# Hybrid trunk on one core: hi and lo of a moving operand side by side, and low parts of weights made by adding transfers

## The chip, the cores and the metric

The kernel runs on one core of a Trainium2 chip. Its engines have queues of their own: TensorE (PE; its weight loads are shown apart as PEld), VectorE (DVE), ScalarE (ACT), GpSimd (POOL) and SyncE (SP), which here only issues transfers (DMA). The metric is device time in microseconds (us), the median of several executions. The profile is of one execution, and counts times from the start of its span.

## The reference

Two layers of an encoder trunk over 256 frames of width 1024. In each layer a normed input is projected once, and the columns are shared out among three mixers and their gates:

```python
h = _rms(x, norm_g[l])
proj = h @ w_in[l]
y_a = _gla(gq, gk, gv, ga, ...) * silu(gz)
y_b = _dsa(bq, bk, bv, iq, ik, iw, ...) * silu(bz)
y_c = _diff(cq, ck, cv, ...) * silu(cz)
g = sigmoid(gate)
merged = g0 * (y_a @ w_br0) + g1 * (y_b @ w_br1) + g2 * (y_c @ w_br2)
x = x + merged @ w_out[l]
```

`_gla` is gated linear attention in chunks of 64 frames: a state per head is updated from keys and values (`state` in the kernel) and read by the queries (`go`). `_dsa` scores keys with a small indexer, keeps the top 64 for each query and attends over them. `_diff` takes the difference of two softmaxes and applies it to values (`av`). All is float32.

## The kernel before

**Two numbers for one.** A float32 product is made of three products in a reduced format: each operand is split into hi (rounded) and lo (what is left), and hi·hi, hi·lo and lo·hi are summed in PSUM. `mm3` issues the three matmuls. A split is one ACT copy that rounds and one DVE subtraction: `split` for activations, `Stream.split` (lines 165 to 170) for weights.

**Weights.** All weights are cut into units of 128 partitions x 1024 numbers (512 KB), 92 per layer, in the order `ORDER` names them: four units for a block of 512 projected columns, six for `br0` and `br1` (the three branches' output projections, one half of the width each), two for each `out` block. `Stream.load` issues a unit's transfer on SP's queue into one of 5 raw buffers; `Stream.split` makes its hi (`whi`) on ACT and its lo (`wlo`) on DVE, each in one of 6 buffers, so that a unit can be split only when PE has finished the unit six back.

**The main line and the tasks.** `project` walks a block's units: for each, two slices of 128 rows, and for each slice three matmuls of 512 columns for each half of the 256 frames (`t` = 0, 1), six in all, and then one `flow.pump()`. `project_T` (for `iq` and `bz`) makes the transposed product with 256 moving columns: for each of four blocks of output columns it walks all four units, so that these four are free late. The rest of a layer (norms, logits, softmax, top-k, the state, the gated read) is written as tasks, Python generators that `flow.pump()` lets go one step at a time; the table `Y` says after how many pumps a step follows. `flow.until` pumps until a result needed by the main line (`y0`, `y1`, `y2` of the branches) is there. A planner orders each engine's instructions from modelled durations and hands out buffers; a task's matmuls may come later than the main line's matmul at which they were issued, not earlier.

**Buffers.** SBUF tiles of one tag share a number of slots: `kp` (27 slots of 128x512) holds gates, value tiles, split queries, the y tiles and the merged output; `w2` (6) is for short-lived work. PSUM has two tags of four banks each: `pj` for projections, `at` for the tasks.

**What the change touches.** `av` (line 608) multiplies the transposed probabilities with cv for each head and block of keys. `gla_task` (line 803) makes the state for each half, splits it into S, then makes `go`, whose squares and scaling give `ya`. `dsa_out` (line 663) is the other use of values; it has its own matmuls and isn't changed. `val[c]` (line 935) splits bv, cv and gv after their projection. `branches` (line 873) takes br0 or br1, branch by branch in the order 0, 2, 1, and frees three gates.

Of the kernel before, what the change touches and what calls it, by code (L numbers as in the profile page):

```python
# [8 lines left out]
F32 = mybir.dt.float32  # L9
F32R = mybir.dt.float32r  # L10
BF16 = mybir.dt.bfloat16
AF = mybir.ActivationFunctionType
OP = mybir.AluOpType
# [5 lines left out]
P = 128  # L19
NOSYNC = mybir.DependencyInfo(mybir.DependencyClass.NoSync, mybir.DependencyReason.DATA)  # L20
CH = 512
# [9 lines left out]
COL = dict(gq=0, gk=256, gv=512, ga=1024, gz=1040, bq=1552, bk=2064, bv=2576, iq=3088, ik=3600,  # L31
           iw=3664, bz=3672, cq=4184, ck=4696, cv=5208, cz=5720, gate=6232)
ORDER = ["bq", "cq", "ck", "gate2", "cz", "bk", "cv", "gq", "iq", "bv", "gv", "gz", "bz", "gate0", "gate3",
         "gate4", "gate5", "br0", "gate1", "br1", "out00", "out10", "out01", "out11"]
BRANCHES = (0, 2, 1)
UNIT, NUNIT = {}, 0
for _c in ORDER:
    UNIT[_c] = NUNIT
    NUNIT += 2 * NB if _c.startswith("br") else 2 if _c.startswith("out") else 4

def columns(*widths):
    at, res = 0, {}
    for name, w in widths:
# [10 lines left out]
MERGE_WAIT = 4  # L56
WARM = 14
AHEAD1 = (0, 2)
Y = dict(sm0=0, qk0=1, qk=3, dsa0=6, dec0=8, diff0=1, gla0=0, att0=3, top=1, blog=6, bpT=11, by=3, clog=4,
         cpT=2, cy=2, za=17, q2=5, st=27, go=9)  # L60
BUFS = dict(w2=6, kp=27, w4=6, ev=2, raw=5, wt=6, ahead=21)


@with_exitstack
def trunk(ctx: ExitStack, tc: tile.TileContext, x0, x1, units, wsmall, pack, ptmp, wa2b, out):
    nc = tc.nc
    V, A, G = nc.vector, nc.scalar, nc.gpsimd

    class Tensor:


        chained, last = False, None
# [14 lines left out]
    TE = Tensor()  # L87
# [3 lines left out]
    sp = ctx.enter_context(tc.tile_pool(name="sp", bufs=1))  # L91
# [4 lines left out]
    def nm(s):  # L96
        cnt[0] += 1
        return f"{s}_{cnt[0]}"

    def w2(shape, dt=F32, n="w2"):  # L100
        return sp.tile(shape, dt, tag="w2", bufs=BUFS["w2"], name=nm(n))

# [15 lines left out]
    def at(shape, n="at"):  # L118
        return pp.tile(shape, F32, tag="at", bufs=4, name=nm(n))
# [22 lines left out]
    class Stream:  # L142
# [22 lines left out]
        def split(self):  # L165
            j = len(self.made)
            raw, (hi, lo) = self.raws[j], self.tiles()
            self.splits[j] = (A.activation(hi, raw, AF.Copy), V.tensor_sub(lo, raw, hi.bitcast(F32)))  # L168
            if j in self.after:
                self.hold(j, self.after[j])  # L170

# [41 lines left out]
    def mm3(ps, lh, ll, rh, rl, first, last):  # L213
        TE.matmul(ps, lh, rh, start=first, stop=False)
        TE.matmul(ps, lh, rl, start=False, stop=False)
        TE.matmul(ps, ll, rh, start=False, stop=last)

    def rstd(ss, n, dim):
        v, r = tiny(n, "v"), tiny(n, "r")
# [163 lines left out]
    ps = pj([P, CH], "idle")  # L383
# [11 lines left out]
    last = {}  # L395
# [7 lines left out]
    wt = [ws.tiles() for _ in range(4)]  # L403
# [53 lines left out]
    r = scale(1)  # L457
# [6 lines left out]
    for l in range(L):  # L464
# [13 lines left out]
        def cq_task(mark, ps, dst):  # L478
            n = headnorm(ps, 8, 64)
            yield Y["qk"]  # L480
            ps, gain = transposed(n), gains[:, L + l:L + l + 1]
# [7 lines left out]
        def ck_task(mark, ps, tt):  # L489
            n = headnorm(ps, 8, 64)  # L490
            yield Y["qk"]
            ps, gain = transposed(n), pkc("dkg", l, l + 1)
# [7 lines left out]
        def qk_task(mark, ps, nh, dh, gain, hi, lo):  # L500
            n = headnorm(ps, nh, dh)
            yield Y["qk"]
            qkT(n, gain, hi, lo)
# [103 lines left out]

        def av(pT, vs, t):

            o = at([P, 4, P], "av")  # L610
            for h in range(4):
                hs = slice(h * P, h * P + P)
                for s in range(t + 1):
                    mm3(o[:, h], *pT[h][s], vs[s][0][:, hs], vs[s][1][:, hs], s == 0, s == t)
            return o

        def transposed_probs(pt, h0, per, t, pT):

# [127 lines left out]
        Es, kd, q2T = [], [], []  # L746
# [56 lines left out]
        def gla_task():  # L803
            carry = None
            S, o = [], []
            for t in range(2):
                sps = at([P, 4, P], "state")
                for h in range(4):
                    lh = kd[t][0][:, h].rearrange("p c d -> p (c d)")
                    ll = kd[t][1][:, h].rearrange("p c d -> p (c d)")  # L810
                    hs = slice(h * P, h * P + P)
                    mm3(sps[:, h], lh, ll, val["gv"][t][0][:, hs], val["gv"][t][1][:, hs], True, True)
                if t == 0:
                    carry = w2([P, 4, P], F32, "carry")
                    A.activation(carry[0:64], sps[64:P], AF.Copy)
                    A.activation(carry[64:P], sps[64:P], AF.Copy)
                    S.append(split(sps, [P, 4, P], "S"))
                else:
                    sd = w2([P, 4, P], F32, "sd")
                    V.tensor_tensor(sd, carry, decay.unsqueeze(2).to_broadcast([P, 4, P]), op=OP.mult)  # L820
                    V.tensor_tensor(sd, sps, sd, op=OP.add)
                    S.append(split(sd, [P, 4, P], "S"))
                yield 1
            ys = []
            for t in range(2):
                yield 1
                o = at([P, 4, P], "go")
                for h in range(4):
                    mm3(o[:, h], q2T[t][0][:, h], q2T[t][1][:, h], S[t][0][:, h], S[t][1][:, h], True, True)
                ss = tiny(4, "ss")  # L830
                junk = w2([P, CH], F32, "junk")
                for h in range(4):
                    A.activation(junk[:, h * P:(h + 1) * P], o[:, h], AF.Square, scale=0.125, accum_out=ss[:, h:h + 1])
                r = rstd(ss, 4, 128)
                f = tiny(4, "f")
                V.tensor_scalar_mul(f, r, 0.125 * 0.5)
                y = w2([P, CH], F32, "ya")
                for h in range(4):
                    hs = slice(h * P, h * P + P)
                    V.scalar_tensor_tensor(y[:, hs], o[:, h], f[:, h:h + 1], val["gz"][t][:, hs], op0=OP.mult, op1=OP.mult)  # L840
                ys.append(y)
            for t in range(2):
                yield Y["go"]
                yTs[0, t] = yT(ys[t])
                flow.done.add(f"y0{t}")


        notsel, val, th, mT = {}, {}, {}, {}
        bpT = [[w4([P, 4, T], F32R, "bpT") for _ in range(2)], [w2([P, 4, P], F32R, "bpT") for _ in range(2)]]
# [44 lines left out]
        for c in ORDER:  # L894
            if c.startswith("out"):
                break
            if c.startswith("br"):
                branches(int(c[2]))
                continue
            if c == "bz":  # L900
                val[c] = [silu2(ps.rearrange("p j t -> p (j t)"), c) for ps in project_T(c)]
                flow.done.add(c)
                continue
            if c == "iq":
                iqT = [split_iq(ps) for ps in project_T(c)]
                flow.done.add(c)
                continue
            ps_ = next(firsts) if c in ORDER[:2] else proj(c, base)
            if c == "bq":
                with ExitStack() as behind:  # L910
                    if l == 0:
                        for e in "AV":
                            behind.enter_context(tc.issue_after(last[e].ins))
                    load_small()
                    if l == 0:
                        constants()
                flow.start(small_task(), Y["sm0"])
            if c in heads:
                nh, dh, gain, dst = heads[c]
                for t in range(2):  # L920
                    flow.start(qk_task(f"{c}{t}", ps_[t], nh, dh, gain, *dst[t]), Y["qk0"])
            elif c == "cq":
                for t in range(2):
                    flow.start(cq_task(f"{c}{t}", ps_[t], cqT[t]), Y["qk0"])
            elif c == "ck":
                for t in range(2):
                    flow.start(ck_task(f"{c}{t}", ps_[t], tts[t]), Y["qk0"])
            elif c == "gq":
                flow.start(gqk_task(ps_), 0, {"dec"})
            elif c.startswith("gate"):  # L930
                for t in range(2):
                    th[int(c[4]), t] = kp([P, CH], F32, "gate")
                    A.activation(th[int(c[4]), t], ps_[t], AF.Tanh, scale=0.5)
            elif c[1] == "v":
                val[c] = [split(ps, [P, CH], c, kp) for ps in ps_]
                flow.done.add(c)
            else:
                val[c] = [silu2(ps, c) for ps in ps_]
                if c == "gz":
                    for g in val[c]:  # L940
                        g3 = g.rearrange("p (h d) -> p h d", h=4)
                        G.tensor_tensor(g3, g3, pkc("glag", l * P, l * P + P).unsqueeze(1).to_broadcast([P, 4, P]),
                                        op=OP.mult)
                flow.done.add(c)
# [3 lines left out]
        for h, n, t in ((0, 0, 0), (0, 0, 1), (0, 1, 0), (0, 1, 1), (1, 0, 0), (1, 1, 0), (1, 0, 1), (1, 1, 1)):  # L948
# [3 lines left out]
            for ps, c in cols:  # L952
                for k in range(4):
                    wh, wl = ws.need(base + UNIT[f"out{n}{h}"] + k // 2)
                    hi, lo = mT[h, t]
# [90 lines left out]
```

## Time and profile before

| | |
|---|---|
| median of 3 runs | 601.77 us (601.76 to 601.82) |
| profiled execution, its own time | 601.7 us |
| its span | 599.8 us |
| busy: PE, weight loads, DVE, ACT, POOL | 593.6, 504.4, 438.6, 348.8, 66.5 us |
| HBM read, written | 99.23, 1.05 MB |

The span is what the rows of the profile cover; the execution's own time is some 2 us longer. A row names line, engine, operation, and what is written from what (out<-in, without buffer numbers; for a matmul the moving operand and then the stationary one). "xN" counts instructions, "busy" sums their durations, "mean" is one instruction's, and what follows the bar's second field is the idle time of the engine before them with the instruction that ended it. Durations of matmuls overlap, as they are pipelined; the spacing of their starts is read from the chain. All matmuls issued through the helper class stand under line 82 and are told apart by their tiles.

### The profile page before, as it was taken

The numbers are of one execution on the slowest core, as the hardware profiler recorded it, in microseconds if no ns is written. First come the engines' busy times: TensorE is split into PE (matmuls) and PEld (weight loads), VectorE is DVE, ScalarE is ACT, GpSimd is POOL, SyncE is SP. The second block draws the span as 40 slices with busy tenths as digits, with TensorE's granted clock in tenths as the row PEclk, the third lists the DMA queues.
The fourth block names the chain that finished last, engine by engine and source line by source line (L and its number), as shares of the span: only waits on it lengthen the run. The fifth ranks groups of instructions, "written<-read, shape, count | busy, mean of one in ns | idle before, by whom it ended". The sixth has DMA issues, their size and how long they took to land.

```text
span 599.8 us, 8713 instructions
## 1 busy us (share of the span) xinstructions
PE 593.6 (99%) x3166; PEld 504.4 (84%) x3166; DVE 438.6 (73%) x731; ACT 348.8 (58%) x609; POOL 66.5 (11%) x95
## 2 busy tenths in 40 slices
PE   8999999999999999999999999999999999999997
PEld 4788888998899888888878888889888988888886
DVE  6878767776999964857586776676789988557661
ACT  5759955665645655353466787466664646544430
POOL 6034101000020100000010340201000020000000
PEclk9999999999999999999999999999999999999999
DMA  8764665344535545655546455642725265466501
GB/s 337 276 210 141 196 194 192 122 129 152 176 107 172 193 156 179 204 178 178 172 140 210 148 170 182 205 134 78 235 95 197 74 209 176 140 211 185 188 12 71
DMA packets 28266, 100.84 MB, mean 168 GB/s; under 512 B 3136, under 2 KB 3520, under 8 KB 28224
## 3 DMA queue, kind: packets, MB, share of 16 engines
q1 hardware_dynamic: 28224, 100.30, 50.4%
q8 instruction: 25, 0.41, 0.3%
q14 instruction: 17, 0.14, 0.1%
HBM read 99.23 MB, written 1.05 MB: 167 GB/s over the span
## 4 chain that ended last, share of the span: by engine, by line
PE 97%; DVE 1%; DMA 1%; ACT 1%; POOL 0%; issue 0%; SPq 0%
PE gate L82 22%; PE br L82 11%; PE out L82 7%; PE bz L82 4%; PE iq L82 4%; PE gz L82 4%; PE cz L82 4%; PE gv L82 4%; PE gq L82 4%; PE ck L82 4%; PE cv L82 4%; PE bv L82 4%; PE bk L82 4%; PE bq L82 3%; PE cq L82 3%; PE av L82 2%
## 5 line engine op out<-in xcount | busy, mean ns | idle before, releaser
L168 DVE TENSOR_TENSOR wlo<-raw,whi 128x1024 fp32r<-128x1024 f32 x180 | 219.8, 1228 | 83.0 <-ACT whi L168 81.7
L168 ACT ACTIVATE whi<-raw 128x1024 fp32r<-128x1024 f32 x180 | 189.5, 1064 | 135.3 <-PE br L82 37.8
L82 PE MATMUL gate<-whi,hTh 128*128 128x512 f32 x192 | 75.5, 394 | 0.0
L82 PE MATMUL gate<-wlo,hTh 128*128 128x512 f32 x192 | 75.3, 392 | 0.0
L82 PE MATMUL gate<-whi,hTl 128*128 128x512 f32 x192 | 75.3, 392 | 0.0
L82 PEld LDWEIGHTS gate<-whi,hTl 128*128 128x128 f32 x192 | 36.1, 188 | 7.2
L82 PEld LDWEIGHTS gate<-wlo,hTh 128*128 128x128 f32 x192 | 36.1, 188 | 7.1
L82 PEld LDWEIGHTS gate<-whi,hTh 128*128 128x128 f32 x192 | 36.1, 188 | 6.9
L221 POOL TENSOR_TENSOR r<-v,half 128x4 f32<-128x4 f32 (+1 forms) x24 | 34.2, 1426 | 2.0
L220 POOL TENSOR_SCALAR v<-ss 128x4 f32<-128x4 f32 (+1 forms) x24 | 9.7, 404 | 203.8 <-DVE ss L317 98.0
L82 PE MATMUL out<-whi,mTh 128*128 128x512 f32 (+1 forms) x72 | 26.7, 371 | 0.0
L82 PE MATMUL out<-wlo,mTh 128*128 128x512 f32 (+1 forms) x72 | 26.3, 366 | 0.0
L82 PE MATMUL out<-whi,mTl 128*128 128x512 f32 (+1 forms) x72 | 26.2, 366 | 0.0
L82 PE MATMUL br<-whi,yTh 128*128 128x512 f32 x64 | 24.9, 389 | 0.0
L82 PE MATMUL br<-wlo,yTh 128*128 128x512 f32 x64 | 24.9, 389 | 0.0
L82 PE MATMUL br<-whi,yTl 128*128 128x512 f32 x64 | 24.9, 389 | 0.0
L82 PE MATMUL iq<-hTh,whi 128*128 128x256 f32 x64 | 18.7, 292 | 0.0
L82 PE MATMUL iq<-hTl,whi 128*128 128x256 f32 x64 | 18.4, 288 | 0.0
L82 PE MATMUL bz<-hTh,whi 128*128 128x256 f32 x64 | 18.4, 287 | 0.0
L82 PE MATMUL iq<-hTh,wlo 128*128 128x256 f32 x64 | 18.3, 287 | 0.0
L82 PE MATMUL bz<-hTl,whi 128*128 128x256 f32 x64 | 18.2, 285 | 0.0
L82 PE MATMUL bz<-hTh,wlo 128*128 128x256 f32 x64 | 18.1, 283 | 0.0
(319 smaller groups left out, 1491.7 us busy)
## 6 DMA issues: line engine op xcount, KB each, us to landing
raw<-in_units SPq DMA_DIRECT2D x184, 512.0 KB, 3.4
wsr<-in_wsmall SPq DMA_DIRECT2D x2, 416.0 KB, 7.5
xe<-in_x SPq DMA_DIRECT2D x1, 584.0 KB, 3.4
x<-in_x SPq DMA_DIRECT2D x1, 512.0 KB, 8.0
out<-xe SPq DMA_DIRECT2D x2, 256.0 KB, 2.0
pt<-in_ptmp SPq DMA_DIRECT2D x1, 384.0 KB, 9.7
wa<-in_wa2b SPq DMA_DIRECT2D x1, 256.0 KB, 6.5
out<-x SPq DMA_DIRECT2D x1, 256.0 KB, 2.0
```

The source lines that it names most:

```text
L82: return self.put(nc.tensor.matmul(*a, **k))
L168: self.splits[j] = (A.activation(hi, raw, AF.Copy), V.tensor_sub(lo, raw, hi.bitcast(F32)))
L220: G.tensor_scalar(v, ss, 1.0 / dim, EPS, op0=OP.mult, op1=OP.add)
L221: G.tensor_tensor(r, v, half[:, :n], op=OP.pow)
```

## The change

Three things are changed together.

1. `mm2` takes the place of `mm3` in `state`, `go` and `av`. The moving operand's hi and lo lie in one tile (`split2`, tag `pair`, 6 slots), and one matmul with the stationary hi takes both, 256 columns, into two halves of a PSUM tile; a second with the stationary lo takes the moving hi and adds to the first half. `both` then adds the halves: an ACT copy of the second half to SBUF and a DVE addition, for each of two PSUM tiles. What follows reads the sum from SBUF.
2. From cv up to gate0 each third unit (9 in a layer, 18 in all) gets its lo without DVE: ACT writes the negated rounded unit into lo, then the rounded unit into hi, and POOL issues a transfer of the unit from HBM that adds to lo.
3. br0 is moved ahead of gate5, `kp` has 21 slots instead of 27, two entries of `Y` are 3 higher, and the scratch for transfers issued by POOL is 1024 instead of 4096.

```diff
 ORDER = [...
-         "gate4", "gate5", "br0", "gate1", "br1", ...]
+         "gate4", "br0", "gate5", "gate1", "br1", ...]
+BY_TRANSFER = UNIT["cv"], UNIT["gate0"]
-Y = dict(..., blog=6, ..., q2=5, ...)
-BUFS = dict(w2=6, kp=27, w4=6, ...)
+Y = dict(..., blog=9, ..., q2=8, ...)
+BUFS = dict(w2=6, kp=21, pair=6, w4=6, ...)
...
         def split(self):
-            self.splits[j] = (A.activation(hi, raw, AF.Copy), V.tensor_sub(lo, raw, hi.bitcast(F32)))
+            if BY_TRANSFER[0] <= j % NUNIT < BY_TRANSFER[1] and j % 3 == 1:
+                a = A.activation(lo, raw, AF.Copy, scale=-1.0)
+                self.splits[j] = (A.activation(hi, raw, AF.Copy), a)
+                G.dma_start(lo, units[j], accum_op=OP.add)
+            else:
+                self.splits[j] = (A.activation(hi, raw, AF.Copy), V.tensor_sub(lo, raw, hi.bitcast(F32)))
...
+    def mm2(ps, lh, ll, r, first, last):
+        if not last or first:
+            TE.matmul(ps, lh, r, start=first, stop=False)
+        TE.matmul(ps[:, 0], ll, r[:, 0], start=False, stop=first and last)
+        if last and not first:
+            TE.matmul(ps, lh, r, start=False, stop=True)
+    def both(ps, o):
+        for i, p in enumerate(ps):
+            A.activation(o[:, 2 * i:2 * i + 2], p[:, :, 1], AF.Copy)
+            V.tensor_tensor(o[:, 2 * i:2 * i + 2], p[:, :, 0], o[:, 2 * i:2 * i + 2], op=OP.add)
+        return o
+    def split2(ps, shape, n):
+        t = pair(shape, n)
+        A.activation(t[:, 0], ps, AF.Copy)
+        V.tensor_sub(t[:, 1], ps, t[:, 0].bitcast(F32))
+        return t
...
         def av(pT, vs, t):
-            o = at([P, 4, P], "av")
+            ps = [at([P, 2, 2, P], "av") for _ in range(2)]
...
-                    mm3(o[:, h], *pT[h][s], vs[s][0][:, hs], vs[s][1][:, hs], s == 0, s == t)
+                    mm2(ps[h // 2][:, h % 2], *pT[h][s], vs[s][:, :, h * P:h * P + P], s == 0, s == t)
+            return both(ps, w2([P, 4, P], F32, "o"))
...
         def gla_task():
-                sps = at([P, 4, P], "state")
+                ps = [(pj if t else at)([P, 2, 2, P], "state") for _ in range(2)]
...
-                    mm3(sps[:, h], lh, ll, val["gv"][t][0][:, hs], val["gv"][t][1][:, hs], True, True)
+                    mm2(ps[h // 2][:, h % 2], lh, ll, val["gv"][t][:, :, h * P:h * P + P], True, True)
+                sps = both(ps, w2([P, 4, P], F32, "state"))
...
-                o = at([P, 4, P], "go")
+                ps = [at([P, 2, 2, P], "go") for _ in range(2)]
...
-                    mm3(o[:, h], q2T[t][0][:, h], q2T[t][1][:, h], S[t][0][:, h], S[t][1][:, h], True, True)
+                    mm2(ps[h // 2][:, h % 2], q2T[t][0][:, h], q2T[t][1][:, h], S[t][:, :, h], True, True)
+                o = both(ps, w2([P, 4, P], F32, "o"))
...
-                val[c] = [split(ps, [P, CH], c, kp) for ps in ps_]
+                val[c] = [split(ps, [P, CH], c, kp) if c == "bv" else split2(ps, [CH], c) for ps in ps_]
...
-    nc = bacc.Bacc(..., dynamic_dma_scratch_size=4096)
+    nc = bacc.Bacc(..., dynamic_dma_scratch_size=1024)
```

More of the change, by code (lines that the diff above doesn't have):

```diff
@@ L33 @@
 ORDER = ["bq", "cq", "ck", "gate2", "cz", "bk", "cv", "gq", "iq", "bv", "gv", "gz", "bz", "gate0", "gate3",
-         "gate4", "gate5", "br0", "gate1", "br1", "out00", "out10", "out01", "out11"]
+         "gate4", "br0", "gate5", "gate1", "br1", "out00", "out10", "out01", "out11"]
 BRANCHES = (0, 2, 1)
@@ L58 @@
 AHEAD1 = (0, 2)
-Y = dict(sm0=0, qk0=1, qk=3, dsa0=6, dec0=8, diff0=1, gla0=0, att0=3, top=1, blog=6, bpT=11, by=3, clog=4,
-         cpT=2, cy=2, za=17, q2=5, st=27, go=9)
-BUFS = dict(w2=6, kp=27, w4=6, ev=2, raw=5, wt=6, ahead=21)
+Y = dict(sm0=0, qk0=1, qk=3, dsa0=6, dec0=8, diff0=1, gla0=0, att0=3, top=1, blog=9, bpT=11, by=3, clog=4,
+         cpT=2, cy=2, za=17, q2=8, st=27, go=9)
+BUFS = dict(w2=6, kp=21, pair=6, w4=6, ev=2, raw=5, wt=6, ahead=21)
 @with_exitstack
@@ L216, in mm3, with pair @@
         TE.matmul(ps, ll, rh, start=False, stop=last)
+    def mm2(ps, lh, ll, r, first, last):
[9 more added lines that the diff above has]
+        return o
+    def pair(shape, n):
+        return sp.tile([P, 2] + shape, F32R, tag="pair", bufs=BUFS["pair"], name=nm(n))
+    def split2(ps, shape, n):
[3 more added lines that the diff above has]
+        return t
     def rstd(ss, n, dim):
@@ L608, in av @@
         def av(pT, vs, t):
-            o = at([P, 4, P], "av")
+            ps = [at([P, 2, 2, P], "av") for _ in range(2)]
             for h in range(4):
-                hs = slice(h * P, h * P + P)
                 for s in range(t + 1):
-                    mm3(o[:, h], *pT[h][s], vs[s][0][:, hs], vs[s][1][:, hs], s == 0, s == t)
-            return o
+                    mm2(ps[h // 2][:, h % 2], *pT[h][s], vs[s][:, :, h * P:h * P + P], s == 0, s == t)
+            return both(ps, w2([P, 4, P], F32, "o"))
         def transposed_probs(pt, h0, per, t, pT):
@@ L810, in gla_task @@
                     ll = kd[t][1][:, h].rearrange("p c d -> p (c d)")
-                    hs = slice(h * P, h * P + P)
-                    mm3(sps[:, h], lh, ll, val["gv"][t][0][:, hs], val["gv"][t][1][:, hs], True, True)
+                    mm2(ps[h // 2][:, h % 2], lh, ll, val["gv"][t][:, :, h * P:h * P + P], True, True)
+                sps = both(ps, w2([P, 4, P], F32, "state"))
                 if t == 0:
@@ L816, in gla_task @@
                     A.activation(carry[64:P], sps[64:P], AF.Copy)
-                    S.append(split(sps, [P, 4, P], "S"))
+                    S.append(split2(sps, [4, P], "S"))
                 else:
@@ L821, in gla_task @@
                     V.tensor_tensor(sd, sps, sd, op=OP.add)
-                    S.append(split(sd, [P, 4, P], "S"))
+                    S.append(split2(sd, [4, P], "S"))
                 yield 1
@@ L1033 @@
     from concourse.bass_utils import run_bass_kernel_spmd as run
-    nc = bacc.Bacc("TRN2", target_bir_lowering=False, num_devices=1, dynamic_dma_scratch_size=4096)
+    nc = bacc.Bacc("TRN2", target_bir_lowering=False, num_devices=1, dynamic_dma_scratch_size=1024)
     arrays, args = {}, []
```

## The prediction

> **What bounds the kernel now.** I read the first page from the top: busy time by engine, the slices, the chain that ended last.
>
> ```profile
> span 599.8 us, 8713 instructions
> PE 593.6 (99%) x3166; PEld 504.4 (84%) x3166; DVE 438.6 (73%) x731; ACT 348.8 (58%) x609; POOL 66.5 (11%) x95
> ...
> PE 97%; DVE 1%; DMA 1%; ACT 1%; POOL 0%; issue 0%; SPq 0%
> ```
>
> TensorE (PE) is busy for 99% of the span, and 97% of the chain is its own; all others have 18 us of it. A busy PE need not be a PE at its best, so I went on to the chain in order of time, where a piece's length over its count is the spacing of consecutive matmuls. In it the pieces of PE follow one another. So the time falls by what leaves PE's queue, and rises by any wait put into it. Nothing that VectorE (DVE) or ScalarE (ACT) saves counts unless PE was waiting for it.
>
> **The change, part 1: fewer matmuls.** Pieces of the chain (start, length, what, count):
>
> ```profile
> 170.35 1.29 PE state L82 x12
> ...
> 219.07 2.23 PE av L82 x20
> 221.31 14.57 PE gate L82 x64
> 235.88 16.32 PE br L82 x72
> ...
> 405.56 1.43 PE iq L82 x12
> ...
> 432.55 1.07 PE av L82 x10
> ...
> 482.49 1.49 PE blog L82 x12
> ```
>
> State, go and the `av` at 432.55 are threes of matmuls with 128 moving columns: state's spacing is 1.29/12 = 107.5 ns, that of `av` 1.07/10 = 107.0; a three costs 322. With 256 columns (`iq`) the spacing is 1.43/12 = 119 ns, so twice the columns cost 11% more, and taking two matmuls of 128 into one of 256 is nearly a matmul for nothing. How many threes there are stands in the groups by shape, where each of the three kinds has this count:
>
> ```profile
> L82 PE MATMUL state<-gvh,kdh 128*128 128x128 f32 x16 | 4.2, 261 | 0.0
> ...
> L82 PE MATMUL go<-Sh,q2Th 128*128 128x128 f32 x16 | 4.2, 261 | 0.0
> ...
> L82 PE MATMUL av<-cvh,pTh 128*128 128x128 f32 x24 | 6.6, 273 | 0.0
> ```
>
> 16 + 16 + 24 = 56 threes become 56 pairs, one matmul of 256 and one of 128. The pair itself is not in the trace. Its dearest bound is the slowest 256 spacing shown (blog, 1.49/12 = 124) plus 107 = 231; its cheapest is two at 107 = 214. The `av` at 219.07 (the other branch's, unchanged) already mixes widths of 256 and 128: 2.23/20 = 111.5 each, 223 a pair. I take that. Gain: 56 x (322 - 223) = 5.5 us, bounds 5.1 and 6.0.
>
> [...]
>
> The two halves must now be added: `both` issues two ACT copies and two DVE adds of 128x256 for each of 12 outputs (2 layers, 3 kinds, 2 halves of the sequence). Nearest rows, and those of the weight units:
>
> ```profile
> L658 ACT ACTIVATE bpT<-pT 128x256 fp32r<-128x256 f32 x8 | 2.9, 386 | 2.0 <-PE pT L85 1.9
> ...
> L790 DVE TENSOR_TENSOR kf<-gq,E 128x256 f32<-128x256 f32 x8 | 3.0, 418 | 1.8 <-PE pT L85 1.8
> L168 DVE TENSOR_TENSOR wlo<-raw,whi 128x1024 fp32r<-128x1024 f32 x180 | 219.8, 1228 | 83.0 <-ACT whi L168 81.7
> ...
> L168 ACT ACTIVATE whi<-raw 128x1024 fp32r<-128x1024 f32 x180 | 189.5, 1064 | 135.3 <-PE br L82 37.8
> ```
>
> 24 x 0.386 = 9.3 us of ACT and 24 x 0.418 = 10.0 of DVE, about 1.6 us in a row per output. I cost them at nothing: PE's main line of projections hides them, since what follows an output (squares, scaling, transposes) is issued by the flow of tasks steps later. Were that cover gone, it would be 12 x 1.6 = 19 us. Two banks of PSUM are held instead of one, but only until the adds, no longer through squares and scaling. Pair tiles for cv, gv and S cost the same copies and subtractions as before.
>
> **Part 2: eighteen low parts by transfer.** Per unit DVE loses 1.228 us, ACT gains 1.064, POOL issues a transfer that adds the unit to its negated high part. Over all: DVE 438.6 - 22.1 + 10.0 = 426.5, ACT 348.8 + 19.2 + 9.3 = 377; neither becomes the bound. The DVE saving is worth nothing, as DVE holds up nothing on the chain. What counts is whether a low part lands before PE wants it. The lead is the time from the unit's first ACT copy (which starts when PE frees the buffer six units back) to PE's first use of the low part. The three shortest leads of the eighteen and, last, the fourth, each a row of ACT and one of PE (for the second, the first of four ACT copies; PE reaches bv's third unit after 24 matmuls of bv):
>
> ```profile
> 400.00 1.10 ACT L168 ACTIVATE whi<-raw 128x1024 fp32r<-128x1024 f32 x1
> 408.22 0.28 PE L82 MATMUL iq<-hTh,wlo 128*128 128x256 f32 x1
> 417.89 3.91 ACT L168 ACTIVATE whi<-raw 128x1024 fp32r<-128x1024 f32 x4
> 425.22 0.39 PE L82 MATMUL bv<-wlo,hTh 128*128 128x512 f32 x1
> 150.72 1.09 ACT L168 ACTIVATE whi<-raw 128x1024 fp32r<-128x1024 f32 x1
> 162.14 0.39 PE L82 MATMUL gz<-wlo,hTh 128*128 128x512 f32 x1
> 370.98 1.06 ACT L168 ACTIVATE whi<-raw 128x1024 fp32r<-128x1024 f32 x1 [1.20 <-issue]
> 384.56 0.39 PE L82 MATMUL cv<-wlo,hTh 128*128 128x512 f32 x1
> ```
>
> Less 1.06 for the negated copy, the transfer has 7.2 us at iq's last unit of layer 2, 6.3 at bv's third, 10.4 at gz's third in layer 1, and 12.5 or more at all others. iq and bz walk through all four units for each block of columns and free them late, which is why the first two are short. No row shows an adding transfer. Issues of plain ones (count, KB, median us to landing), two steps of POOL, and what DVE did during the first of them:
>
> ```profile
> raw<-in_units SPq DMA_DIRECT2D x184, 512.0 KB, 3.4
> pk<-in_pack SPq DMA_DIRECT2D x1, 133.0 KB, 9.8
> 37.86 1.18 POOL L220 TENSOR_SCALAR v<-ss 128x4 f32<-128x4 f32 x1 [3.31 <-DVE iws L538]
> ...
> 41.54 0.20 POOL L220 TENSOR_SCALAR v<-ss 128x8 f32<-128x8 f32 x1 [1.41 <-DVE ss L317]
> 37.77 1.22 DVE L168 TENSOR_TENSOR wlo<-raw,whi 128x1024 fp32r<-128x1024 f32 x1
> ```
>
> For POOL's share I bound 0.2 to 1.2 us and take 1.0. For the way from issue to landing the bounds are 3.4 (the same bytes from the same place) and 9.8 (waiting among other loads); the adding reads two places, so I go from the nearest row most of the way to the middle (6.6) and take 6.0. Together T = 7.0, bounds 3.6 and 11.0. PE's wait is the sum of what T exceeds each lead by: 0.7 at T = 7 (bv only); 2.6 at 8; 6.6 at 10; 9.2 at 11.0, when gz's unit is late too. I take 0.7.
>
> [...]
>
> The transfers add 18 x 512 KB to the 184 x 512 KB of the loads, on the same 16 engines; SP's queue is not touched. On POOL, a transfer waits for ACT's negated copy, and behind it stand the v and r of the norms, the memsets of q and acc and the gz scaling; POOL works 66.5 of 599.8 us, and DVE's qn and ACT's squares wait at most a few us more, inside the pumps between tasks.
>
> **Part 3: order and buffers.** Moving br0 ahead of gate5 starts it 48 matmuls earlier (at 14.57/64 = 0.228 us each 10.9 us, so near 225 instead of 235.88), but its third branch needs the last y only another 48 matmuls on. The `av` at 219.07 ends at 221.3, so that y, one scaling and one split of 0.7 us steps later, is there near 224: cover about 12 us. The later dues (three steps of six matmuls, 4.1 us) fit into it. Cost nothing; without cover, up to 4 us a layer. The kp slots fall from 27 to 21 while cv and gv give back 8 only in mid-layer; see the rivals.
>
> **Sum.** The profiled execution took 601.7 us (span 599.8 and 1.9 around it), the median of the runs 601.77. 601.7 - 5.5 + 0.7 = 596.9, on the runs' scale 597.0.
>
> **Rivals.** (a) *Late low parts*, slower: from T = 9.5 the waits at iq's last and bv's third unit eat the whole gain. At T = 10.8 (1.0 and the 9.8 row) they are 3.6 + 4.5 + 0.4 = 8.5: 604.7. For it: nothing in the trace adds in a transfer, and POOL can be held. Against: the raw row's 3.4, and fifteen leads of 12.5 us or more. A mechanism that lengthens T is in the POOL rows above: v takes 0.20 us at 41.54, but 1.18 at 37.86, where it runs beside DVE's subtraction of two SBUF tiles. One such hold brings T to 8.0 and the time to 598.8. [...]
>
> (b) *Too few kp slots*: near the end of a layer I count gates 3, 5 and 1 (6), the three y (12) and mT (4): 22 for 21, so gate1's second half waits in PSUM for the first third of br1. PE needs that bank only two projections later; I price it at 0.5 to 1.5 us a layer: 598 to 600. For it: the count. Against: the planner can place the evacuation by its own plan.
>
> (c) *The pair isn't cheaper*: the moving operand's two halves lie 512 columns apart in cv, gv and S, while every 256-wide row shown reads one run. If it cost two matmuls, the gain is nil: 601.7 + 0.7 = 602.4. Against it, the 119 ns of iq show columns are not what is paid for.
>
> **Chances.** Forecast (595.9 to 597.6) 0.48; better, towards 6.0 and no wait, 0.06; smaller gain through (b) or T near 8 (597.6 to 600.5) 0.18; (c) or gain and waits cancelling 0.10; (a) 0.18. A measurement of this kernel tells 0.2%, 1.2 us, from no change. So faster 0.72, same 0.10, slower 0.18. Range 595.3 to 604.5: below it the cheapest bound, above it half of (a).
>
> **What would show it.** Right: PE with 56 matmuls and 56 weight loads fewer, pair spacing near 111 ns, PE still 97% of the chain, ACT near 377 us and DVE near 427. Part 2 wrong: PE or its weight load waiting for an adding transfer at iq's or bv's units, and its issue row above 9 us. (b): a late gate copy with PE idle before br1. Wrong altogether if PE gaps appear where no low part is due, through a plan made for other durations.

## The result, and the profile after

The changed kernel took 609.06 us (median of four: 607.15, 608.75, 609.37, 610.12) against 601.80 before: a ratio of 1.0115, 95% interval 1.0103 to 1.0127. I had forecast 597.0 in 595.3 to 604.5. The change is slower. Its profiled execution is the one of 607.15 us. Its first page (busy time, then shares of the chain that ended last):

```profile
span 605.4 us, 8689 instructions
...
PE 589.9 (97%) x3110; PEld 498.0 (82%) x3110; DVE 428.0 (71%) x737; ACT 373.2 (62%) x651; POOL 82.9 (14%) x113
...
PE 59%; DMA 1%; ACT 1%; issue 0%; DVE 0%; ACTq 0%
```

As forecast, 56 matmuls and 56 weight loads are gone, and DVE and ACT stand within 4 us of what I had worked out. The chain of after can be followed back only to 231.66 us, so its shares add up to 62% of the span, and its 59% is not to be set beside the 97% of before. What has changed is that TensorE is busy for 97% of the span where it was for 99%. What it waited for (total us, times, longest):

```profile
PE gate L84 <- ACT gate L966: 3.5, 2, 2.6
PE br L84 <- ACT gate L966: 2.2, 1, 2.2
PE bv L84 <- DMA wlo<-in_units: 2.2, 1, 2.2
...
PE gv L84 <- DVE iqo L593: 0.7, 1, 0.7
```

Before, all waits of this view lie at the first blocks of the first layer, and none of these four was there:

```profile
PE bq L82 <- DVE wlo L411: 1.3, 2, 0.7
PE idle L82 <- DVE idle L382: 1.2, 1, 1.2
PE qkT L85 <- DVE qn L320: 0.2, 1, 0.2
```

L966 is the gate's tanh, which copies a finished accumulator out of PSUM. The chain (start, length, what, count) prices the pair and shows the late low part:

```profile
421.89 7.51 DMA wlo<-in_units
429.40 0.04 issue
429.45 4.38 PE bv L84 x18
...
467.82 0.86 PE state L84 x8
...
485.17 0.87 PE go L84 x8
```

0.86/8 = 107.5 ns a matmul, averaged over 256 and 128 columns by turns, so a pair takes 215 and the 56 together give 56 x 107.5 = 6.0 us. From the profiled execution before: 601.7 - 6.0 + 8.6 (the four rows of waits) = 604.3. The other 2.9 us are small waits and the restarts behind the long ones: TensorE's gaps, measured as starts of matmuls against the median spacing of their shape, are together 11.8 us more than before, and 601.7 - 6.0 + 11.8 = 607.5.

**Why the tanh is late.** ScalarE before (start, length, operation), and then TensorE before, where the last row is the first matmul of gate 4, which takes over the PSUM bank of gate 0:

```profile
206.25 0.61 ACT L227 ACTIVATE yTh<-yT 128x512 fp32r<-128x512 f32 x1
206.73 1.11 ACT L933 ACTIVATE gate<-gate 128x512 f32<-128x512 f32 x2
```

```profile
209.56 0.39 PE L82 MATMUL gate<-whi,hTl 128*128 128x512 f32 x1
209.79 0.38 PE L85 MATMUL pT<-xe,bp 128*128 128x128 f32 x2
209.93 0.47 PE L82 MATMUL gate<-whi,hTh 128*128 128x512 f32 x1
```

The same two places after:

```profile
207.09 0.60 ACT L260 ACTIVATE yTh<-yT 128x512 fp32r<-128x512 f32 x1 [1.57 <-PE yT L87]
207.58 0.47 ACT L639 ACTIVATE bp<-blog,negm 128x256 f32<-128x256 f32 x1
...
208.03 0.47 ACT L639 ACTIVATE bp<-blog,negm 128x256 f32<-128x256 f32 x1
...
208.48 1.09 ACT L966 ACTIVATE gate<-gate 128x512 f32<-128x512 f32 x2
```

```profile
207.82 0.40 PE L84 MATMUL gate<-whi,hTl 128*128 128x512 f32 x1
209.14 0.50 PE L84 MATMUL gate<-whi,hTh 128*128 128x512 f32 x1 [0.92 <-ACT gate L966]
```

In both kernels gate 0's two tanh stand on ScalarE behind `yTh`, the end of a task: go, its squares and scaling, the transposes of `ya`. Before, they follow at once; after, two softmax steps of the other branch (`bp`, with short rows of their sums) stand between as well. Before, the first tanh ended near 207.3, and TensorE wanted the bank at 209.93: a margin of 2.6 us, which no row of waits shows. After, the tanh comes 1.75 us later: 0.84 as `yTh` starts later, 0.9 by the two softmax steps. TensorE wants the bank at about 208.05 (207.82 and one spacing of 0.23), 1.9 us earlier, as it has had fewer matmuls to do. The margin is eaten from both sides, and the wait here is 0.9 us. The longest one, 2.6 us, is at the same place of layer 2, where `yTh` starts at 505.26 and the tanh at 507.60.

### The profile page after: what moved, and what is told of

Same layout as the page of the kernel before. It is cut to its first block, busy times and chain, and to the rows that moved or that the text cites. A ratio compares the mean times of both kernels' runs of the same rounds, so it can differ in the third digit from the quotient of the medians.

```text
span 605.4 us, 8689 instructions
## 1 busy us (share of the span) xinstructions
PE 589.9 (97%) x3110; PEld 498.0 (82%) x3110; DVE 428.0 (71%) x737; ACT 373.2 (62%) x651; POOL 82.9 (14%) x113
## 4 chain that ended last, share of the span: by engine, by line
PE 59%; DMA 1%; ACT 1%; issue 0%; DVE 0%; ACTq 0%
PE gate L84 14%; PE br L84 10%; PE out L84 7%; PE bz L84 2%; PE bq L84 2%; PE gv L84 2%; PE gz L84 2%; PE gq L84 2%; PE cz L84 2%; PE ck L84 2%; PE cv L84 2%; PE cq L84 2%; PE bk L84 2%; PE iq L84 2%; DMA wlo<-in_units 1%; PE bv L84 1%
## 5 line engine op out<-in xcount | busy, mean ns | idle before, releaser
L175 DVE TENSOR_TENSOR wlo<-raw,whi 128x1024 fp32r<-128x1024 f32 x162 | 198.3, 1230 | 73.2 <-ACT whi L175 71.9
L173 POOL DMA_DIRECT2D wlo<-in_units x18 | 16.3, 903 | 112.4 <-ACT wlo L171 97.1
L171 ACT ACTIVATE wlo<-raw 128x1024 fp32r<-128x1024 f32 x18 | 19.1, 1059 | 10.2 <-PE bv L84 4.0
```

The costliest lines, as they stand in the source:

```text
L171: a = A.activation(lo, raw, AF.Copy, scale=-1.0)
L173: G.dma_start(lo, units[j], accum_op=OP.add)
```

## The experiments

Theories. T: the adding transfers come late and cost the time. P: the new places (br0, the two pauses) or the 21 slots do. T fell, and P held for some 2 us only. The other letters (Q, R, C, S, G and V) are theories too, each told in the expectation where it first stands. Each time is a median, with the ratio to the kernel before and its 95% interval.

### Parts alone, and parts undone

**All low parts by VectorE**, else as the changed kernel:

```diff
-            if BY_TRANSFER[0] <= j % NUNIT < BY_TRANSFER[1] and j % 3 == 1:
+            if False:
```

> The changed kernel, but all low parts of the weights are made by VectorE again; the pairs, the order of the branches, the pauses and the 21 slots stay. The pairs are worth 56 x 107.5 ns = 6.0 us by the rows of after. Theory T (all that was lost comes from the adding transfers, the gate waits too): 601.8 - 6.0 = 595.8 us, and TensorE's gaps at the gates are gone. Theory P (the gate waits, 1.1 + 2.4 + 2.7 = 6.2 us in the profile of after, come from the new places of br0, the second logits and q2, or from 21 slots): about 602 us, with these gaps still there and only the gaps at bv and before gv gone.

613.54 us, 1.0200 (1.0182 to 1.0218): slower still by 4.5 us. Theory T falls, and the transfers are found to help. The waits:

```profile
PE gate L84 <- ACT gate L966: 6.3, 2, 3.6
PE gv L84 <- DVE iqo L593: 4.2, 2, 2.1
```

The wait at gv has grown from 0.7 to 4.2 us: `iqo` is the last piece of the split of iq, which frees the banks gv needs, and VectorE has more to do there (nine more subtractions in a layer, 1.23 us each). It isn't VectorE's load alone: on ScalarE, too, the split of iq stands behind a `yTh`, here at 138.12 us and in the changed kernel at 133.67.

**The transfers alone**: the kernel before with the new branch of `Stream.split` and nothing else.

> The kernel before with the 18 adding transfers alone: no pairs, old order and pauses, 27 slots. Theory T: the transfers cost all that is missing, 601.8 + 6.0 + 7.3 = about 615 us. Theory P: they cost the gaps at bv and before gv only, 2.35 + 0.94 = 3.3 us in the profiled execution, up to 7 us where transfers are slower: 605 to 609 us. My prediction's own sum gave 0.7 us for them: 602.5 us.

602.03 us, 1.0000 (0.9990 to 1.0009). They cost nothing that can be measured, less than both theories said. Its waits, all of them:

```profile
PE bq L83 <- DVE wlo L417: 1.2, 2, 0.6
PE idle L83 <- DVE idle L388: 1.2, 1, 1.2
PE qkT L86 <- DVE qn L326: 0.2, 1, 0.2
```

**The places alone**: the kernel before with br0 ahead of gate5 and the pauses 9 and 8.

> The kernel before with br0 ahead of gate5, the pause of the logits at 9 and that of q2 at 8, nothing else (27 slots, no pairs, no transfers). Theory T: 601.8 us. Theory P by the places: 608 us, with gaps of 1 to 3 us at gate3, gate4 and br0. Theory P by the slots: 601.8 us.

603.74 us, 1.0039 (1.0025 to 1.0053): 1.9 us, not 6, and no gate wait, though the softmax steps stand ahead of gate 0's tanh here too.

**25 slots**: the changed kernel with `kp=25, pair=4`.

> The changed kernel with 25 slots in place of 21 and 4 pair buffers in place of 6. Theory P by the slots: the gate waits go, 609.1 - 6.2 = about 603 us, unless 4 pair buffers make a wait of their own at state or av. Theory T and P by the places: 609 us, the gate gaps stay.

607.78 us, 1.0110 (1.0077 to 1.0144). The gate waits stay (2.6 us at gates, 2.2 at br). The number of slots is not the cause.

### Moving a tile out of the shared slots

**Gate 0 alone** (no transfers, kp 19):

```diff
-                    th[int(c[4]), t] = kp([P, CH], F32, "gate")
+                    th[int(c[4]), t] = (sp.tile([P, CH], F32, tag="g0", bufs=2, name=nm("gate"))
+                                        if c[4] in "0" else kp([P, CH], F32, "gate"))
```

> As the kernel with pairs and no transfers (613.5 us), but gate 0's two tanh tiles have two slots of their own, and kp has 19. In all kernels so far ScalarE's order has these tanh behind the hi copy of yT, which was allocated from kp before them. Theory Q (slots of a tag are handed out in program order; a tile of the main line that is allocated behind a task's tile has its work ordered behind the task, so PE's accumulator comes free only when the task is through; the sums of hi and lo made that task later): the two waits of TensorE on the gate tanh, 3.8 + 0.4 and 2.8 + 0.4, go, as does some clock lost behind them: 605 to 607 us; the waits at gv, 2.3 each, stay. Theory R (ScalarE and VectorE have too much to do in that stage for the sums to fit): the wait only changes its place, 612 us or more.

615.44 us, 1.0236 (1.0216 to 1.0256). The order did change (its tanh is now built ahead of the first sum of go) and its wait went, but that at br grew and that at gv stayed (small ones, 1.6 us at bz and 0.9 at av, are new):

```profile
PE br L84 <- ACT gate L967: 5.3, 4, 2.2
PE gv L84 <- DVE iqo L593: 4.2, 2, 2.1
```

Taken alone this spoke for theory R: gates 3 and 4, still in kp, stand behind `yTh` and `ybh`, and br waits for them.

**iq's split alone** (no transfers): `iqe` and `iqo` in four slots of their own instead of w2, `pair=4`.

> As the kernel with pairs and no transfers (613.5 us), but iq's four split tiles have four slots of their own outside w2, and pair has 4 slots. In that kernel gv's first matmul waits 2.3 us a layer for iqo, which stands on ScalarE and VectorE behind yTh, which waits for the transposes of yc. Theory Q (iq's split stands behind the task because w2's six slots now also hold the sums): the two waits at gv go, 2 x (2.3 + 0.2) = 5 us, 608 to 609 us; the waits at the gates stay. Theory R: about 613 us, with a wait elsewhere in the stretch of bv and gv.

610.13 us, 1.0143 (1.0128 to 1.0158): 3.4 of the 5 us expected; the gv waits went, though VectorE had no less to do, so the late `iqo` is a matter of order too. New waits of 0.7 to 1.4 us came at gz and at the gates, and those for gate tanh (2.4 us at gates, 4.0 at br) stayed.

**Both, with the transfers** (kp 19, pair 4).

> The changed kernel with its transfers, with both: gate 0 in two slots of its own (kp 19) and iq's split in four (pair 4). Theory Q: from the profiled 607.15 the waits 1.1 and 2.7 at gate 0's tanh and 0.9 before gv go: 602.4 us; 2.4 us at the tanh of gate 4 behind ybh and 2.35 us at bv's late low part stay. Theory R: 607 to 609 us.

609.68 us, 1.0124 (1.0108 to 1.0140): no gain over the changed kernel; the waits are at br (3.4), bv (2.1) and bz (1.6).

**Both, with the old places** (kp 21, pair 3).

> As the kernel with both sorts of own slots and transfers, but with br0 behind gate5 and the pauses of before (6 and 5), with kp 21, and pair cut to 3 slots to make room. The places alone cost 1.9 us without pairs, so Theory Q gives about 2 us less than its neighbour, 600.5 us, less still (598) if gate 4's tanh comes in time there; if 3 pair slots make S or av wait, a wait of TensorE at state, go or av shows and the time is up to 3 us higher. Theory R: no gain over its neighbour.

604.48 us, 1.0037 (1.0020 to 1.0053): 5.2 us better than its neighbour. What is left is 4.0 us at the tanh of gate 3, which stands behind `ybh`, and 1.2 at bv. (The neighbour also had two slots of kp fewer and one pair slot more.)

### The sums, and four edits at once

The sum of the halves can be one VectorE step, a reduction that reads both halves from PSUM:

```diff
-            A.activation(o[:, 2 * i:2 * i + 2], p[:, :, 1], AF.Copy)
-            V.tensor_tensor(o[:, 2 * i:2 * i + 2], p[:, :, 0], o[:, 2 * i:2 * i + 2], op=OP.add)
+            V.tensor_reduce(o[:, 2 * i:2 * i + 2], p.rearrange("p h b n -> p h n b"), axis=AX, op=OP.add)
```

**In the kernel without transfers:**

> As the kernel with pairs, new places, 21 slots and no transfers (613.5 us), but hi and lo halves are added in one VectorE step (a reduction over the two halves, read from one PSUM tile) in place of a ScalarE copy and a VectorE addition. Theory C (the sums lengthen the task chains, and the copies of main-line accumulators that are ordered behind these chains come late): TensorE's waits at gv (2 x 2.3) and at the gates (3.8 + 2.8) shrink by half or more, 605 to 609 us. Theory S (two PSUM tiles for one, the pair slots, or the 21 slots make the waits, not the sums): 612 to 614 us.

617.38 us, 1.0251 (1.0218 to 1.0284): not better, so Theory C falls as I had put it. gv's wait for `iqo` rose to 6.6 us: for half an output ScalarE loses a copy of 0.38 us, but VectorE's one step takes 0.68 us (rows of the one-step kernels below) where its addition took 0.42.

**The first part of the change alone**: pairs in 3 slots, two-step sums, old places, kp 27, no transfers.

> The first part of the change alone: the kernel before with pairs (in 3 slots) and their sums, with the old places, 27 slots and no transfers. My prediction's sum for this part is 601.7 - 5.5 = 596.2 us. If the pairs with their sums bring waits by themselves, 603 to 608 us, with waits at the gate tanh and at gv; if the loss needs the new places or 21 slots, under 600 us.

610.12 us, 1.0123 (1.0101 to 1.0146). So the waits come with the pairs, their sums and what goes with them (two PSUM tiles for an output, pair slots); neither the places nor 21 slots are needed:

```profile
PE gate L84 <- ACT gate L966: 7.5, 4, 2.0
...
PE gv L84 <- DVE iqo L593: 1.4, 2, 0.7
```

**The same with one-step sums.**

> The same with the sums in one VectorE step. Theory C: 3 to 6 us less than its neighbour with two steps. Theory S: the same within 1 us.

621.02 us, 1.0316 (1.0274 to 1.0359), against both theories. Here a task itself holds TensorE, and the sum of go is late in VectorE's queue:

```profile
PE gate L84 <- ACT gate L965: 8.5, 4, 2.5
PE gv L84 <- DVE iqo L592: 3.8, 2, 1.9
PE yT L87 <- DVE o L237: 2.7, 1, 2.7
```

**Four edits**: gates 0, 3 and 4 in six slots of their own (kp 21, pair 3), one-step sums, old places, transfers but for bv's units.

> Pairs with one-step sums, the old places, 21 slots and 3 pair slots, the tanh of gates 0, 3 and 4 in six slots of their own, and the transfers but for those of bv. Theory C: the waits on gate tanh and on the late low part are gone, 601.8 - 6.0 = 595.8 plus at most 2 us of small waits, 596 to 598. Theory S: 602 to 606.

596.19 us, 0.9904 (0.9889 to 0.9919): faster than both kernels. It still has two PSUM tiles for each output, 3 pair slots and 21 kp slots, so theory S falls: these alone make no wait. Busy times, and all its waits:

```profile
PE 588.1 (99%) x3110; PEld 498.9 (84%) x3110; DVE 435.8 (73%) x739; ACT 364.3 (61%) x625; POOL 80.3 (14%) x111
```

```profile
PE bq L84 <- DVE wlo L443: 1.6, 2, 1.0
PE idle L84 <- DVE idle L414: 1.2, 1, 1.2
PE qkT L87 <- DVE qn L352: 0.2, 1, 0.2
```

ScalarE in it, gate 0's two tanh and `yTh`: the first tanh starts as soon as TensorE is through, over 14 us ahead of `yTh`.

```profile
195.49 0.60 ACT L966 ACTIVATE gate<-gate 128x512 f32<-128x512 f32 x1 [3.35 <-PE gate L84]
...
198.10 0.58 ACT L966 ACTIVATE gate<-gate 128x512 f32<-128x512 f32 x1
...
209.85 0.60 ACT L259 ACTIVATE yTh<-yT 128x512 fp32r<-128x512 f32 x1
```

### One thing taken back at a time from 596.19

**All low parts by VectorE** (`if False` as above):

> The kernel at 596.2 us, but with all low parts made by VectorE. Theory V (VectorE's extra work lets the split of iq, and with it gv, come late; the transfers took that work away): the wait at gv for iqo returns, 2 to 3.5 us a layer, and costs some clock: 600 to 604 us. Theory G (only the gates' slots matter): 595.5 to 597 us.

602.68 us, 1.0004 (0.9995 to 1.0014): +6.5. This is what theory V says; of its new waits this is the main one:

```profile
PE gv L84 <- DVE iqo L592: 3.8, 2, 1.9
```

**Sums in two steps:**

> The kernel at 596.2 us, but with the sums in two steps as in the change (ScalarE copies, VectorE adds). Theory G and theory V: 595.5 to 597.5 us, as one step was no faster in the earlier pair of runs (617.4 against 613.5 without own slots). Theory C (length of the chain): up to 602 us, with waits at gates.

596.70 us, 0.9909 (0.9894 to 0.9924): +0.5. Once the gates have slots of their own and VectorE has the transfers' help, the sums are as good as free, in either form.

**Gates back in kp** (27 slots, the same room):

> The kernel at 596.2 us, but with the gates in kp again, which has 27 slots (the same room in all). Theory G: ScalarE's order has the tanh of gate 0 behind yTh again and that of gate 3 behind ybh; TensorE waits for them as it did in the pairs alone, 1.9 + 2.2 us a layer, and loses some clock: 603 to 608 us. Theory V: no more than 598 us, as 16 subtractions fewer a layer end in time.

609.28 us, 1.0116 (1.0097 to 1.0135): +13.1, as theory G said and more. Its main wait, and ScalarE's order:

```profile
PE gate L84 <- ACT gate L965: 8.7, 4, 2.8
```

```profile
207.84 0.58 ACT L259 ACTIVATE yTh<-yT 128x512 fp32r<-128x512 f32 x1
208.31 1.07 ACT L965 ACTIVATE gate<-gate 128x512 f32<-128x512 f32 x2
```

**The new places:**

> The kernel at 596.2 us, but with br0 ahead of gate5 and the pauses 9 and 8 of the change. The places cost 1.9 us without pairs and 5.2 us between the two kernels with own slots: 598 to 602 us, with waits at br0 for the tanh of gate 4 and for m. If they cost only where gates stand behind tasks: 596 to 597 us.

598.50 us, 0.9939 (0.9924 to 0.9954): +2.3, close to the 1.9 without pairs and within what was expected, but not by the waits I had named: br0 has none. The new waits are gv's, 0.9 us in two, for low parts by transfer, and 0.4 at the first layer's start.

**The changed kernel with the gates' slots alone** (six own, kp 21, pair 3):

> The changed kernel with one thing altered: gates 0, 3 and 4 have six slots of their own (pair has 3 slots, kp 21). Theory G: the waits at the gates go; what stays is the places (2.3 us over 596.2), the two steps (0.5) and bv's late low part (2.3): about 601 us. Theory that the waits only move, as they did with gate 0 alone: 606 to 610 us.

602.68 us, 1.0004 (0.9985 to 1.0024): 6.4 us better than the change, and as fast as before (its ten runs spread from 599.7 to 604.6). The waits for gate tanh fell from 5.7 us to 0.7 and did not move elsewhere; 2.4 us at bv and 0.7 at gv stayed.

**bv's low parts by transfer too:**

> The kernel at 596.2 us with bv's low parts by transfer too, as in the change. My prediction's sum gave bv's wait 0.7 us, the profile of the changed kernel 2.35 us: 596.9 by the one, 598 to 599 by the other, with one wait of TensorE for an adding transfer at bv in layer 2. If later instructions have slack that takes it up, 596.2 us.

600.73 us, 0.9968 (0.9953 to 0.9984): +4.5, more than both figures. TensorE waits once, for bv's third unit of layer 2:

```profile
PE bv L84 <- DMA wlo<-in_units: 3.0, 1, 3.0
```

The prices add up: 596.2 + 2.3 (places) + 0.5 (two steps) + 4.5 (bv) = 603.5, against 602.7 measured for the slots-only kernel, which differs from 596.2 in these three. Slots of their own for the gates, without pairs, were not run; before, no gate wait is there to win.

## Why the prediction was wrong

- **Part 1, matmuls: right.** 56 gone; 215 ns a pair where I took 223, so 6.0 us where I said 5.5, the cheap end of my bounds. Rival (c) falls. The gain was there to be had: 601.8 - 596.2 = 5.6 us.
- **`both` at nothing: this step failed.** I said TensorE's main line hides the sums, "since what follows an output (squares, scaling, transposes) is issued by the flow of tasks steps later". I looked only at what follows in the task. But copies of the main line stand behind the task's end on ScalarE, and these TensorE needs: the pairs alone bring 7.5 us of waits for gate tanh. The bound I gave "were that cover gone", 19 us, held; the claim that the cover was there did not. The before profile had shown the margin, 2.6 us at gate 0 of layer 1, in the rows on ScalarE's order that I did not read. The cause in the code is that the gates share a tag's slots with tasks: own slots changed the order and took the waits away, giving them back returned both, and the waits were there with 21, 25 and 27 slots. That slots are handed out in the order of the program, so that the tanh may not come ahead of the task, explains this, but was not tested by itself. How much of the delay is the sums' own time stays open as well: with shorter sums (one step) the pairs alone got slower, not faster.
- **DVE's saving "worth nothing": this failed too.** It is worth nothing before (602.03 against 601.80), where TensorE waits for VectorE at the first blocks only. Once the sums are on VectorE, gv waits for `iqo`, and the transfers save 4.5 to 6.5 us. Slots of its own for iq's split took that wait away as well, so what the transfers help is again something that stands behind a task.
- **Part 2, lateness: right place, too small.** bv's third unit of layer 2 was the late one, as I had ranked it. But alone in the kernel before the same transfers met no wait, so it was late only together with the rest of the change; why was not followed up. The chain of after shows 7.51 us there, counted from the start of POOL's issue, so POOL's share is in it, and 0.40 us between ScalarE's copy and the issue: 7.9 us where my T was 7.0 (1.0 and 6.0). The rows of issues (median), counted the same way, show it too:

```profile
raw<-in_units SPq DMA_DIRECT2D x184, 512.0 KB, 4.2
wlo<-in_units POOLq DMA_DIRECT2D x18, 512.0 KB, 8.3
```

  POOL's own share was well chosen: 903 ns an issue in the groups of after against my 1.0 us; the way to landing was the term too small. PE's wait was 2.2 us instead of 0.7, so the lead came out shorter as well, 5.7 us for my 6.3. In the cleanest setting it cost 4.5 us of time. Rival (a) is right on this one unit and not the main cause of the loss: without any transfer the changed kernel is slower still.
- **Part 3, places at nothing: too low** by 1.9 us (alone) to 2.3, and by up to 5.2 where gates still shared slots.
- **Rival (b), slots: near, and wrong in the mechanism.** I counted slots and priced 0.5 to 1.5 us a layer at br1. The waits are at gate 4 and br0, and come from the sharing of the tag, not from the count.
- **What would show it:** "PE gaps appear where no low part is due, through a plan made for other durations" is what came; that the planner's durations are to blame I cannot show. I had no price on it.

## What to carry to other kernels

When the main engine has no gaps, look for its margins before taking work from it: for each accumulator, when its copy out ends and when its bank is wanted again. Here TensorE, with fewer matmuls to do, wanted gate 0's bank 1.9 us sooner, and the tanh that stood behind the delayed task came 1.75 us later. Give tiles that the main line waits for slots of their own, and then take edits back one at a time: here the same pairs with the same sums cost 8.3 us alone and won 5.1 (596.70) with own slots for three gates and sixteen transfers.

## What the runs showed of the hardware

**Behind some waits of 2 to 3 us TensorE ran at half its clock for some microseconds.** Time windows of the kernel with bv's transfers (window, its length, busy us and count of PE, PEld, DVE, ACT and POOL, granted clock of TensorE, DMA share, GB/s):

```profile
422.00:424.00 2.00, 0.42 (x2) 0.00 (x0) 1.82 (x3) 1.98 (x3) 0.91 (x1) 1.00 0.97 365
424.00:426.00 2.00, 0.55 (x1) 0.50 (x2) 0.75 (x1) 0.00 (x0) 0.00 (x0) 0.67 1.07 381
426.00:428.00 2.00, 2.00 (x6) 1.57 (x5) 0.00 (x0) 0.00 (x0) 0.00 (x0) 0.50 0.96 281
428.00:430.00 2.00, 2.00 (x6) 1.52 (x6) 0.00 (x0) 0.30 (x1) 0.00 (x0) 0.50 1.05 250
430.00:432.00 2.00, 2.00 (x7) 1.58 (x6) 0.00 (x0) 1.70 (x2) 0.84 (x1) 0.62 0.85 266
432.00:434.00 2.00, 2.00 (x17) 1.83 (x16) 0.91 (x2) 0.94 (x2) 0.03 (x1) 1.00 0.59 102
```

By the clocks of these rows TensorE had half its clock for 6.8 us, from about 424.7, still in the wait, to about 431.5. In the chain bv's seventeen matmuls behind the wait, from 425.45 on, took 6.98 us, 0.41 each, where thirty of the kernel before took 6.83, 0.23 each: some 3 us are lost. Not each execution pays this: of the six of this kernel, two ran at a mean clock of 1.000 (598.58 and 599.37), three at 0.997 (600.63 to 600.83) and one, this profile, at 0.993 (602.29). So steps of 0.3%, about 1.8 us, come on top of the wait; 596.2 + 3.0 = 599.2 is near the two at full clock. The changed kernel's four ran at 1.000 (607.15) and 0.997 (608.75 to 610.12). In the profile of the first of these, the clock is 1.00 in each window of 2 us behind the waits of 2.2 us (br, bv) and 2.6 us. In the pairs alone it fell to 0.50 behind a wait of 2.0 us (the same columns, with the wait in the first row):

```profile
226.00:228.00 2.00, 0.36 (x4) 0.22 (x2) 1.90 (x4) 1.37 (x3) 0.00 (x0) 1.00 0.70 225
...
230.00:232.00 2.00, 2.00 (x6) 1.62 (x5) 0.00 (x0) 0.00 (x0) 0.00 (x0) 0.50 0.00 0
```

What sets off the lower clock was not shown. The kernel before, whose profile has no wait above 1.2 us, ran at 0.996 or 0.997 in three of the thirteen executions taken beside the kernel with the new places (602.71 to 602.97).

**Adding transfers** took about twice as long as plain ones of the same size: 8.3 us from the start of the issue to landing (median of 18) against 4.2, in the same execution; the plain ones took 3.4 in the kernel before. The adding ones are also issued from another queue, POOL's, and no run tells the two apart.
